# A hybrid token mixer on one core: weights kept split from the first block on, a second x tile, and zeroed tiles in the weight buffers

## The chip, the cores and the metric

One core of a Trainium2 chip runs the kernel. The metric is the device time of one execution in microseconds. The kernel before takes 2813.61 us in the median of three runs (2803.16 to 2818.05).

## The reference

One layer of a diffusion backbone, for 256 context tokens and 2048 latent tokens of width 1024, in float32. Each token is normalised and modulated by a condition, multiplied by w_in (1024 to 2560), and split into ten columns of 256 that feed four mixers; their outputs are multiplied by w_out, added to x with a gate, and an MLP of width 4096 with squared ReLU follows.

```python
def token_mixing(h, hg_s0, s5_s0_re, s5_s0_im, P, l):
    z = jnp.dot(h, P['w_in'][l])
    a_val, a_gate, g_u, g_v, h_q, h_i, h_g, h_ff, h_fb, s5_u = jnp.split(z, N_IN_BLOCKS, axis=-1)
    o_conv = conformer_conv(a_val, a_gate, ...)
    o_gm = chunk_gmlp(g_u, g_v, ...)
    o_hg, hg_end = hgrn_mixer(h_q, h_i, h_g, h_ff, h_fb, ...)
    o_s5, s5_re, s5_im = s5_mixer(s5_u, ...)
    mixed = jnp.concatenate([o_conv, o_gm, o_hg, o_s5], axis=-1)
    return jnp.dot(mixed, P['w_out'][l]), hg_end, s5_re, s5_im
...
    x = x + g1 * mix
    h = rms_norm(x, P['norm2_g'][l]) * (1.0 + sc2) + sh2
    x = x + g2 * jnp.dot(jnp.square(jax.nn.relu(jnp.dot(h, P['mlp_w1'][l]))), P['mlp_w2'][l])
```

The part that matters here is the hgrn mixer: a gated recurrence with a 64x64 state per head, run forward and backward. Its scores inside a chunk are q·k with a decay between the two positions.

## The kernel before

Tokens are cut into five blocks: block 0 holds the 256 context tokens, blocks 1 to 4 hold 512 latent tokens each. Activations lie with channels on the partitions. Every large product is made in split precision: a float32 operand is cut into a high part and a low rest, and three matmuls (hi·hi, hi·lo, lo·hi) add up; lines L192 to L194 (`gemm_cm`), L579 to L581 (`gemm_tm`) and L1114 to L1116.

A weight unit is 128 x 1024 numbers, 0.5 MB. It is loaded into a raw buffer (tile `wraw`, three buffers, L179), and split by ScalarE (L156, the high part) and GpSimd or VectorE (L160, L162, the rest) into a tile `whl` of 1 MB (four buffers). The first use writes the split tile to DRAM (`kept_unit`, L182); later uses read that (L176). w_p1t and w_p1c are the weights of the first pass, w_p2c and w_p2t those of the second.

The first pass takes the blocks in the order 1, 2, 3, 4, 0 (`P1_ORDER`). Block 1 has a function of its own (`first_block`, from L655), in which its products go along with the ada modulation, k slice by k slice: `load(k)` fetches a slice of the ada weights (tile `aw`, two buffers) and of the first weights, `ready(k)` computes the modulation of that slice (adaT, L657), modulates x and splits the weights. These eight splits take the first two units of w_p1c and all four of w_p1t; they are not kept. For each later block x is loaded, squared and its rms found (`pass1_x`, tile `x`; L240, L248, L252, L256, L289), `pass1_h` modulates and splits it, `pass1_t` makes four token-major tiles (v and the S5 input; tile `vt` has two buffers), and `pass1_g` makes three groups for each of two pairs of heads.

Each of the ten (block, pair) combinations has an hgrn chain, `hgrn_local`. It goes through seven levels in which the decays of neighbouring spans double their length: at each level ScalarE copies q into a zeroed tile (L794, L795), PE makes scores of q and kt (L762, 32 columns each), and VectorE and GpSimd multiply kt, q and the decays by neighbours (L804, L805, L806, L813). Levels 0 to 2 use three tiles `qz0` to `qz2` that all chains share and that are zeroed once (L1395); levels 3 to 6 use `qzr`, zeroed each time. Level 4 copies the scores of five levels by a mask (L820). A chain ends with transposes (L830), the product with v (L836) and the state contributions (L845). Chain i + 1 starts when chain i has done five steps, so two chains run interleaved. When all are done for a segment, `hgrn_states` runs the recurrence over chunks (L869, L872).

The second pass takes block 0 first and then 1 to 4; its first block loads w_p2c and w_p2t raw, splits them and keeps them: ten units. w_out and the MLP follow. A scheduler with a model of the engines turns the program into one fixed order per engine, before the kernel runs; the DMAs are all issued by SyncE (SP) in its own fixed order, and an SP row that waits for a semaphore holds up all rows behind it.

Of the kernel before, what the change touches and what calls it, by code (L numbers as in the profile page):

```python
# [10 lines left out]
F32 = mybir.dt.float32  # L11
F32R = mybir.dt.float32r
# [38 lines left out]
P1_ORDER = [1, 2, 3, 4, 0]  # L51
# [23 lines left out]
def trunk_kernel(ctx, tc, I, O):  # L75
# [31 lines left out]
    def f32(ap):  # L107
        return ap.bitcast(F32)
# [41 lines left out]
    def wtile():  # L150
        return wts.tile([128, 2, 1024], F32R, tag="whl", name=nm("whl"), bufs=4)
# [17 lines left out]

    kept = {}  # L170

    def kept_unit(name, i, pool_only=True, every=3, keep=True):

        t = wtile()
        if (name, i) in kept:
            SP.dma_start(f32(t), f32(kept[name, i]))  # L176
            return t[:, 0, :], t[:, 1, :]
        raw = wts.tile([128, 1024], F32, tag="wraw", name=nm("wraw"), bufs=3)
        SP.dma_start(raw, I[name][i])  # L179
        split_unit(raw, pool_only, every=every, t=t)  # L180
        kept[name, i] = dt_(f"{name}_hl{i}", [128, 2, 1024], F32R)
        SP.dma_start(f32(kept[name, i]), f32(t))  # L182
        return t[:, 0, :], t[:, 1, :]

    def gemm_cm(ps, n, unit, hs, ts=None):
# [18 lines left out]
    def dt_(name, shape, dt=F32):  # L204
        return dram.tile(shape, dt, tag=name, name=name)
# [363 lines left out]
        pass1_save(b, hs)  # L569
        return hs  # L570

    def pass1_x(b, xp):
        x8 = xblock(xp, b, w=512, halves=4)
        return x8, rms_rstd(xp, x8, BLOCKS[b][1], V)

    def gemm_tm(ps, w, xs, wh, wl, first, last):
# [83 lines left out]
    def first_block(b, adap, xp, hp, p1):  # L660


        t0, n, c = BLOCKS[b]
        m = n // CH
        w = 512 + 2 * 128

        def load(k):
            aw = adap.tile([128, 8, 256], F32, tag="aw", name=nm("aw"), bufs=2)
            SP.dma_start(aw, I["ada_w0"][k])
            raw = wts.tile([128, 1024], F32, tag="wraw", name=nm("wraw"), bufs=3)  # L670
            SP.dma_start(raw[:, 0:512], I["w_p1t"][k // 2][:, (k % 2) * 512:(k % 2) * 512 + 512])
            SP.dma_start(raw[:, 512:w].rearrange("p (u f) -> p u f", u=2),
                         I["w_p1c"][0:2, :, k * 128:(k + 1) * 128].rearrange("u p f -> p u f"))
            return aw, raw

        c32 = cond32(adap)
        x8 = xblock(xp, b, w=512, halves=4, engs=(V, G, V), pos=True)
        loads = [load(k) for k in range(4)]
        yield
        ps = pg()  # L680
        for k in range(0, 8, 2):
            sq = [xp.tile([128, 512], F32, tag=tag, name=nm("sq"), bufs=2) for tag in ("sq", "hm")]
            for i in range(2):
                A.activation(sq[i][:, :n], x8[:, k + i, :n], AF.Square)
            V.tensor_tensor(sq[0][:, :n], sq[0][:, :n], sq[1][:, :n], ALU.add)
            PE.matmul(ps[:, :n], ones, sq[0][:, :n], start=k == 0, stop=k == 6)
        rstd = rstd_of(ps, n, 1.0 / D_MODEL)
        yield
        pts, pcs = None, None
        hs, ws_ = [], []  # L690

        def ready(k):
            aw, raw = loads[k]
            ada_unit(pa(), (aw[:, 0:4], aw[:, 4:8]), c32, adap, slice(k, k + 9, 8))
            V.scalar_tensor_tensor(gs1[:, :, k], adaT[:, 8 + k, :], 1.0, n1g[:, k:k + 1].to_broadcast([128, 2]),
                                   ALU.add, ALU.mult)
            hs.append(modulate1(xp, hp, x8, n, rstd, gs1[:, c, :], adaT[:, 0:8, c], k))
            ws_.append(split_unit(raw, True, w))

        ready(0)  # L700
        for k in range(8):
            if k < 7:
                ready(k + 1)
            hi, lo = ws_[k]
            if k == 0:
                pts = [psums["w"].tile([128, 512], F32, tag="pw", name=nm("pw")) for _ in range(m - 1)] + [pg()]
                pcs = [pg(), pg()]
            for i in range(m):
                gemm_tm(pts[i], 512, [x[:, i * 128:(i + 1) * 128] for x in hs[k]], hi[:, 0:512], lo[:, 0:512],
                        k == 0, k == 7)  # L710
            for i in range(2):
                ws = slice(512 + 128 * i, 640 + 128 * i)
                PE.matmul(pcs[i][:, :n], hi[:, ws], hs[k][0][:, :n], start=k == 0, stop=False)
                PE.matmul(pcs[i][:, :n], hi[:, ws], hs[k][1][:, :n], start=False, stop=False)
                PE.matmul(pcs[i][:, :n], lo[:, ws], hs[k][0][:, :n], start=False, stop=k == 7)
            if k + 4 < 8:
                loads.append(load(k + 4))
        state0.append((b, pts, pcs, hs, p1))
# [599 lines left out]
    def pool(stack, name, bufs=1, side="left"):  # L1318
        return stack.enter_context(tc.tile_pool(name=name, bufs=bufs, side=side))
# [20 lines left out]
    with ExitStack() as e1:  # L1340
        p1a = pool(e1, "p1a")
        es = ExitStack()
        s5s = pool(es, "s5s")
        s5t = pool(es, "s5t")
        psum(es, t=1)
        with ExitStack() as ea:
            psum(ea, w=3)
            adap = pool(ea, "adap")
            hp = pool(e2, "hp", 8, side="right")
            ex = ExitStack()  # L1350
            xp = pool(ex, "xp", side="right")
            start = first_block(P1_ORDER[0], adap, xp, hp, p1a)
            step(start, 1)
            small = s5_small(s5s)
            more_consts()
            run(start)
            lower_bounds()
            first_out()
        hs, vt, gates = first
        with ExitStack() as e:  # L1360
            psum(e, u=3)
            s5_tables(s5t, scr, small)
        es.close()
        psum(e1, s=2)
        Sx = [spool.tile([128, 4, 4, 64], F32, tag="Sc", name="Sc"),
              spool.tile([128, 4, LAT // CH + 2, 64], F32, tag="Sl", name="Sl")]
        pre = pass1_x(P1_ORDER[1], xp)
        state = [hs, vt, pre]

        def prep(i):  # L1370

            b, pair = P1_ORDER[i // 2], i % 2
            if i == 0:
                g_ = gates
            else:
                if pair == 0:
                    state[1] = pass1_t(b, state[0], p1a)
                g_ = pass1_g(b, pair, state[0], p1a)
            vt = state[1]
            if pair == 1 and i // 2 + 1 < NB:  # L1380
                state[0] = pass1_h(P1_ORDER[i // 2 + 1], xp, hp, state[2])
                if i // 2 + 2 < NB:
                    state[2] = pass1_x(P1_ORDER[i // 2 + 2], xp)
                else:
                    ex.close()
            return g_ + (vt,)

        ready = [prep(0), prep(1)]
        p1 = pool(e1, "p1")
        masks_ = p1.tile([128, 5, 32], I32, tag="masks", name="masks")  # L1390
        for o_ in range(0, 128, 32):
            SP.dma_start(masks_[o_:o_ + 32], I["masks"][o_:o_ + 32, :, o_:o_ + 32])
        qz = [p1.tile([128, 1024], F32, tag=f"qz{lv}", name=f"qz{lv}") for lv in range(3)]
        for z in qz:
            G.memset(z, 0.0)  # L1395
        prev = None
        for i in range(2 * NB):
            cur = hgrn_local(P1_ORDER[i // 2], i % 2, *ready[i], p1, qz, Sx, masks_)
            for _ in range(5):
                step(cur)  # L1400
                if prev:
                    step(prev)
            prev = cur
            if i == 0:
                s5_kernels()
            if i + 2 < 2 * NB:
                ready.append(prep(i + 2))
        run(prev)
        hs = state[0]
        p2 = pool(e2, "p2", side="right")  # L1410
        gm = [const("gmg", [128, 256], I["gmlp_norm_g"], F32, p2, SP),
              const("gmw", [128, 4, 128], I["gmlp_ws"], F32, p2, SP),
              const("gmb", [128, 2, 128], I["gmlp_bs"], F32, p2, SP)]

        def all2():
            gates = []
            for b in P1_ORDER[-1:] + P1_ORDER[:-1]:
                for i, _ in enumerate(pass2(b, p2, hp, hs if b == P1_ORDER[-1] else None, Sx, gates, *gm)):
                    if i in DEFER and b != P1_ORDER[-1]:
                        hgrn_out(*gates.pop(0))  # L1420
                    yield
            for g_ in gates:
                hgrn_out(*g_)

        second = all2()
        step(second, 2)
# [88 lines left out]
    for b in range(1, NB):  # L1515
        x8, h2 = nxt
# [120 lines left out]
```

## Time and profile before

| | |
|---|---|
| median of three runs | 2813.61 us |
| the profiled execution: time, span | 2807.04 us, 2805.3 us |
| granted clock, mean | 0.968 |
| PE busy | 2628.2 us, 94% |
| VectorE (DVE) busy | 1818.5 us, 65% |
| ScalarE (ACT) busy | 1143.9 us, 41% |
| GpSimd (POOL) busy | 911.6 us, 32% |
| DMA | 467.35 MB, mean 167 GB/s |

The busy time of PE counts from the start of a matmul to its modelled end; matmuls overlap, so a sum over groups is more than the time they take. Shares of the whole span hide that the kernel has two halves: up to about 1050 us several engines and the DMA queues take turns in being the last, and after it PE hardly stops. To read a stage, cut it out with a window and see which engine is full there, and what the idle engine waits for.

### The profile page before, as it was taken

Reading aid. Unit: us, or ns where it says so; the run is one execution under the profiler, and the core shown is the slowest. Engines: PE = TensorE matmul, PEld = TensorE weight load, DVE = VectorE, ACT = ScalarE, POOL = GpSimd, SP = SyncE. Lnnn points to the kernel's source line nnn. Section 1 sums busy time; section 2 is a strip of 40 time slices with the busy share of each in tenths; the row PEclk is TensorE's granted clock in tenths of the full one; section 3 lists DMA queues with packets and bytes.
Section 4 is the critical chain, followed back from the end, with each engine's and each line's share of the span. In section 5 each row is a group of like instructions: output and inputs, shape, how many; then the busy total and the mean of one; then the engine's idle time right before and its main releaser. Section 6 shows DMA issues by size and latency. Waiting matters only on the chain.

```text
span 2805.3 us, 44442 instructions
## 1 busy us (share of the span) xinstructions
PE 2628.2 (94%) x17544; PEld 2185.3 (78%) x17544; DVE 1818.5 (65%) x2686; ACT 1143.9 (41%) x1830; POOL 911.6 (32%) x809
## 2 busy tenths in 40 slices
PE   6786989899999889999999999999999999999998
PEld 3665767777777679987788888788887888888888
DVE  9869677856698877569873485944575334643336
ACT  4645555532434545442432343233333223423323
POOL 4346234512534533342221342221432112421113
PEclk8898899899999989999999999999999999999999
DMA  7894556878986756542332343333343233233223
GB/s 265 286 302 155 203 194 198 293 256 307 318 283 228 230 201 202 161 144 83 113 112 92 130 148 113 99 105 115 107 161 100 96 98 128 98 122 100 95 97 128
DMA packets 186865, 467.35 MB, mean 167 GB/s; under 512 B 40864, under 2 KB 70688, under 8 KB 173600
## 3 DMA queue, kind: packets, MB, share of 16 engines
q1 hardware_dynamic: 184496, 463.32, 49.3%
q8 instruction: 139, 2.28, 0.3%
q10 hardware_dynamic: 2160, 1.18, 0.1%
q14 instruction: 70, 0.57, 0.1%
HBM read 383.23 MB, written 77.53 MB: 164 GB/s over the span
## 4 chain that ended last, share of the span: by engine, by line
PE 60%; DVE 11%; DMA 2%; ACT 1%; issue 1%; POOL 1%; SPq 0%; DVEq 0%; ACTq 0%; POOLq 0%
PE pg L193 19%; PE pg L194 19%; PE pg L192 19%; DVE x L1202 4%; DVE m L1013 1%; DVE whl L162 1%; DVE gg L1021 1%; DMA x<-in_xT_dram 0%; DVE sq L1030 0%; DMA x<-uD 0%; DVE lo L304 0%; DMA x<-mixD 0%; DVE pa L289 0%; DVE x L240 0%; DVE lo L1263 0%
## 5 line engine op out<-in xcount | busy, mean ns | idle before, releaser
L192 PE MATMUL pg<-hi,whl 128*128 128x512 f32 (+1 forms) x3488 | 1282.4, 370 | 18.3 <-DMA whl<-w_p1c_hl 5.5
L193 PE MATMUL pg<-lo,whl 128*128 128x512 f32 (+1 forms) x3488 | 1281.3, 368 | 5.1 <-DVE lo L1263 3.6
L194 PE MATMUL pg<-hi,whl 128*128 128x512 f32 (+1 forms) x3488 | 1278.9, 368 | 1.9 <-DVE whl L162 1.7
L160 POOL TENSOR_TENSOR whl<-wraw,whl 128x512 fp32r<-128x512 f32 (+1 forms) x296 | 428.4, 1468 | 1174.3 <-ACT whl L156 1126.4
L192 PEld LDWEIGHTS pg<-hi,whl 128*128 128x128 f32 x3488 | 662.8, 190 | 133.4 <-issue 7.5
L193 PEld LDWEIGHTS pg<-lo,whl 128*128 128x128 f32 x3488 | 662.8, 190 | 117.1 <-issue 8.2
L194 PEld LDWEIGHTS pg<-hi,whl 128*128 128x128 f32 x3488 | 662.3, 190 | 110.6 <-issue 4.6
L156 ACT ACTIVATE whl<-wraw 128x1024 fp32r<-128x1024 f32 (+1 forms) x396 | 415.5, 1051 | 577.6 <-PE pg L194 457.6
L162 DVE TENSOR_TENSOR whl<-wraw,whl 128x1024 fp32r<-128x1024 f32 x248 | 313.7, 1265 | 67.6 <-ACT whl L156 66.7
L1275 DVE SCALAR_TENSOR_TENSOR x<-pg,adaT,x 128x512 f32<-128x512 f32 (+1 forms) x168 | 111.8, 668 | 279.9 <-PE pg L194 279.4
L1260 DVE TENSOR_TENSOR t<-t 128x512 f32<-128x512 f32 (+1 forms) x160 | 113.5, 710 | 246.0 <-ACT t L1259 245.9
L1259 ACT ACTIVATE t<-pg 128x512 f32<-128x512 f32 (+1 forms) x160 | 88.3, 552 | 354.6 <-PE pg L194 354.5
L1202 DVE SCALAR_TENSOR_TENSOR x<-x,cvw 128x512 f32<-128x512 f32 (+1 forms) x300 | 218.8, 774 | 0.2
L1263 DVE TENSOR_TENSOR lo<-t,hi 128x512 fp32r<-128x512 f32 (+1 forms) x160 | 140.5, 879 | 35.6 <-ACT hi L1262 35.5
L804 POOL TENSOR_TENSOR kt<-kt,tnx 64x256 f32<-64x256 f32 (+1 forms) x120 | 94.8, 807 | 157.8 <-issue 116.3
L1262 ACT ACTIVATE hi<-t 128x512 fp32r<-128x512 f32 (+1 forms) x160 | 92.9, 581 | 88.3 <-DVE t L1260 88.3
L252 POOL TENSOR_TENSOR sq<-sq,sq 128x512 f32<-128x512 f32 (+1 forms) x56 | 87.2, 1558 | 122.8 <-ACT sq L248 122.8
L1243 DVE SCALAR_TENSOR_TENSOR x<-pg,adaT,x 128x512 f32<-128x512 f32 (+1 forms) x40 | 27.6, 691 | 105.8 <-PE pg L194 105.8
L804 DVE TENSOR_TENSOR kt<-kt,tnx 64x256 f32<-64x256 f32 (+1 forms) x120 | 59.3, 517 | 52.6 <-PE psc L762 51.8
L248 ACT ACTIVATE sq<-x 128x512 f32<-128x512 f32 (+1 forms) x120 | 65.8, 552 | 63.1 <-DVE sq L252 15.5
L303 ACT ACTIVATE hi<-hm,adaT 128x512 fp32r<-128x512 f32 (+1 forms) x72 | 49.6, 698 | 61.2 <-DVE hm L301 59.9
L304 DVE SCALAR_TENSOR_TENSOR lo<-hm,adaT,hi 128x512 fp32r<-128x512 f32 (+1 forms) x72 | 66.7, 942 | 6.1 <-ACT hi L303 5.2
(376 smaller groups left out, 2762.0 us busy)
## 6 DMA issues: line engine op xcount, KB each, us to landing
wraw<-in_mlp_w_dram SPq DMA_DIRECT2D x328, 512.0 KB, 3.5
whl<-w_p2c_hl SPq DMA_DIRECT2D x32, 1024.0 KB, 7.5
whl<-w_p1c_hl SPq DMA_DIRECT2D x22, 1024.0 KB, 8.5
wraw<-in_w_out_dram SPq DMA_DIRECT2D x40, 512.0 KB, 3.5
awt<-in_ada_w_dram SPq DMA_DIRECT2D x32, 512.0 KB, 6.1
whl<-w_p1t_hl SPq DMA_DIRECT2D x12, 1024.0 KB, 5.6
x<-in_xT_dram SPq DMA_DIRECT2D x16, 512.0 KB, 6.2
aw<-in_ada_w_dram SPq DMA_DIRECT2D x8, 1024.0 KB, 6.6
```

Source lines behind the costliest of these rows:

```text
L156: A.activation(hi[:, :w], raw[:, :w], AF.Copy)
L160: G.tensor_tensor(lo[:, h_], raw[:, h_], f32(hi[:, h_]), ALU.subtract)
L162: V.tensor_tensor(lo[:, :w], raw[:, :w], f32(hi[:, :w]), ALU.subtract)
L192: PE.matmul(ps[:, :n], wh, xh[:, ts], start=k == 0, stop=False)
L193: PE.matmul(ps[:, :n], wh, xl[:, ts], start=False, stop=False)
L194: PE.matmul(ps[:, :n], wl, xh[:, ts], start=False, stop=k == 7)
L804: eng.tensor_tensor(kv, kv, tb(lo_, hi_, 1 - half)[:, hs_, :], ALU.mult)
L1202: V.scalar_tensor_tensor(acc[i][:, :n], u2[:, i, k:k + n], cvw[:, i, k:k + 1], acc[i][:, :n], ALU.mult, ALU.add)
L1260: V.tensor_tensor(r, r, r, ALU.mult)
L1262: A.activation(hi, r, AF.Copy)
L1263: V.tensor_tensor(lo, r, f32(hi), ALU.subtract)
L1275: V.scalar_tensor_tensor(x8[:, o, ts], ps[:, :n], adaT[:, 40 + o, c:c + 1], x8[:, o, ts], ALU.mult, ALU.add)
```

## The change

Four things. (1) The eight splits of `first_block` are written to the kept tiles of w_p1t and w_p1c, in 24 pieces, so later blocks read these units. (2) `pass1_x` puts x8 alternately into a second pool `xq` and the old one. (3) The `pass1_t` of block 2 is called before the chains. (4) The three `qz` tiles are taken from the raw weight buffers (`wraw`, three buffers), and no longer from a pool of their own.

```diff
--- before.py
+++ after.py
@@ -169,6 +169,11 @@
 
     kept = {}
 
+    def kept_tile(name, i):
+        if (name, i) not in kept:
+            kept[name, i] = dt_(f"{name}_hl{i}", [128, 2, 1024], F32R)
+        return kept[name, i]
+
     def kept_unit(name, i, pool_only=True, every=3, keep=True):
 
         t = wtile()
@@ -178,8 +183,7 @@
         raw = wts.tile([128, 1024], F32, tag="wraw", name=nm("wraw"), bufs=3)
         SP.dma_start(raw, I[name][i])
         split_unit(raw, pool_only, every=every, t=t)
-        kept[name, i] = dt_(f"{name}_hl{i}", [128, 2, 1024], F32R)
-        SP.dma_start(f32(kept[name, i]), f32(t))
+        SP.dma_start(f32(kept_tile(name, i)), f32(t))
         return t[:, 0, :], t[:, 1, :]
 
     def gemm_cm(ps, n, unit, hs, ts=None):
@@ -569,8 +573,8 @@
         pass1_save(b, hs)
         return hs
 
-    def pass1_x(b, xp):
-        x8 = xblock(xp, b, w=512, halves=4)
+    def pass1_x(b, xp, xq):
+        x8 = xblock(xq, b, w=512, halves=4)
         return x8, rms_rstd(xp, x8, BLOCKS[b][1], V)
 
     def gemm_tm(ps, w, xs, wh, wl, first, last):
@@ -695,7 +699,12 @@
             V.scalar_tensor_tensor(gs1[:, :, k], adaT[:, 8 + k, :], 1.0, n1g[:, k:k + 1].to_broadcast([128, 2]),
                                    ALU.add, ALU.mult)
             hs.append(modulate1(xp, hp, x8, n, rstd, gs1[:, c, :], adaT[:, 0:8, c], k))
-            ws_.append(split_unit(raw, True, w))
+            t = wtile()
+            ws_.append(split_unit(raw, True, w, t=t))
+            SP.dma_start(f32(kept_tile("w_p1t", k // 2)[:, :, (k % 2) * 512:(k % 2) * 512 + 512]), f32(t[:, :, 0:512]))
+            for u in range(2):
+                SP.dma_start(f32(kept_tile("w_p1c", u)[:, :, k * 128:(k + 1) * 128]),
+                             f32(t[:, :, 512 + 128 * u:640 + 128 * u]))
 
         ready(0)
         for k in range(8):
@@ -1364,8 +1373,11 @@
         psum(e1, s=2)
         Sx = [spool.tile([128, 4, 4, 64], F32, tag="Sc", name="Sc"),
               spool.tile([128, 4, LAT // CH + 2, 64], F32, tag="Sl", name="Sl")]
-        pre = pass1_x(P1_ORDER[1], xp)
+
+        xqs = [pool(ex, "xq", side="right"), xp]
+        pre = pass1_x(P1_ORDER[1], xp, xqs[0])
         state = [hs, vt, pre]
+        early = []
 
         def prep(i):
 
@@ -1374,23 +1386,24 @@
                 g_ = gates
             else:
                 if pair == 0:
-                    state[1] = pass1_t(b, state[0], p1a)
+                    state[1] = early.pop() if early else pass1_t(b, state[0], p1a)
                 g_ = pass1_g(b, pair, state[0], p1a)
             vt = state[1]
             if pair == 1 and i // 2 + 1 < NB:
                 state[0] = pass1_h(P1_ORDER[i // 2 + 1], xp, hp, state[2])
                 if i // 2 + 2 < NB:
-                    state[2] = pass1_x(P1_ORDER[i // 2 + 2], xp)
+                    state[2] = pass1_x(P1_ORDER[i // 2 + 2], xp, xqs[(i // 2 + 1) % 2])
                 else:
                     ex.close()
             return g_ + (vt,)
 
         ready = [prep(0), prep(1)]
+        early.append(pass1_t(P1_ORDER[1], state[0], p1a))
         p1 = pool(e1, "p1")
         masks_ = p1.tile([128, 5, 32], I32, tag="masks", name="masks")
         for o_ in range(0, 128, 32):
             SP.dma_start(masks_[o_:o_ + 32], I["masks"][o_:o_ + 32, :, o_:o_ + 32])
-        qz = [p1.tile([128, 1024], F32, tag=f"qz{lv}", name=f"qz{lv}") for lv in range(3)]
+        qz = [wts.tile([128, 1024], F32, tag="wraw", name=f"qz{lv}", bufs=3) for lv in range(3)]
         for z in qz:
             G.memset(z, 0.0)
         prev = None
```

On SP the writes of (1) stand among the loads of the first block's raw slices and of aw: three for each of the eight units, which read that unit's split tile and wait for its split. Line numbers of the kernel after are 4 to 13 higher.

On PE at the end of block 3's third pass1_t tile, whose last products open each piece. Before:

```order
L581 MATMUL pg_3053<-whl_2992,hi_2542 128x512
L762 MATMUL psc_2613<-q_2604,kt_2603 32x32 x32
L762 MATMUL psc_2653<-qzr_2648,kt_2026 32x32 x32
L762 MATMUL psc_2701<-qz_1541,kt_2603 32x32 x32
L762 MATMUL psc_2747<-qzr_2742,kt_2026 32x32 x32
L762 MATMUL psc_2793<-qz_1542,kt_2603 32x32 x32
L762 MATMUL psc_2839<-qzr_2834,kt_2026 64x64 x16
L762 MATMUL psc_2867<-qz_1543,kt_2603 32x32 x26
L256 MATMUL pa_2598<-sq_2575,ones 128x512
L762 MATMUL psc_2867<-qz_1543,kt_2603 32x32 x6
L830 MATMUL psc_2909<-ident,kt_2026 128x128 x8
L836 MATMUL psc_2919<-at_2028,vt_837 64x128 x8
```

After (L771 is L762 before, L839 and L845 are L830 and L836):

```order
L585 MATMUL pg_3050<-whl_2989,hi_2539 128x512
L771 MATMUL psc_2698<-qz_1699,kt_2600 32x32 x32
L771 MATMUL psc_2744<-qzr_2739,kt_2023 32x32 x32
L771 MATMUL psc_2790<-qz_1700,kt_2600 32x32 x32
L260 MATMUL pa_3761<-sq_3738,ones 128x256
L771 MATMUL psc_2836<-qzr_2831,kt_2023 64x64 x16
L771 MATMUL psc_2864<-qz_1701,kt_2600 32x32 x32
L839 MATMUL psc_2906<-ident,kt_2023 128x128 x8
L845 MATMUL psc_2916<-at_2025,vt_867 64x128 x8
L771 MATMUL psc_2942<-qzr_2937,kt_2600 32x32 x29
L854 MATMUL psc_2916<-vt_867,kt_2023 128x64 x8
```

The chain stands two steps further on when the products end: the first scores (q, and the first qzr) now come ahead, and an rms sum of 256 columns stands where one of 512 stood. Up to the next product 270 scores follow one another before (208 in the rows shown, 62 behind them), and 198 after (173 and 25).

SP, the first load of a raw second-pass unit. Before, and with its waits:

```order
L563 DMA hD_101<-lo_1431 128x512 [waits DMAHW7_49,DVE_49]
L562 DMA hD_101<-hi_1436 128x512 [waits DMAHW0_49,Activation_49]
L563 DMA hD_101<-lo_1437 128x512 [waits DMAHW1_49,DVE_49]
L179 DMA wraw_6573<-in_w_p2c_dram 128x1024 [waits DMAHW2_49]
L562 DMA hD_101<-hi_1442 128x512 [waits DMAHW3_49,Activation_49]
```

After:

```order
L762 DMA q_6200<-qn_5834 64x256 [waits DMAHW0_49]
L762 DMA q_6200<-qn_5834 64x256 [waits DMAHW1_49]
L849 DMA oD_118<-at_5426 128x512 [waits DMAHW2_49,Activation_49]
L184 DMA wraw_6571<-in_w_p2c_dram 128x1024 [waits DMAHW3_49,PE_49,Activation_49]
L835 DMA qD_109<-q_5897 128x512 [waits DMAHW4_49,DVE_49]
L184 DMA wraw_6605<-in_w_p2c_dram 128x1024 [waits PE_49,Activation_49]
```

It moved from row 108 to row 309 and waits for PE and ACT, behind the last chains' stores.

PE, behind the last product of the first pass (pg_5867). After:

```order
L198 MATMUL pg_5867<-hi_4879,whl_5868 128x256
L771 MATMUL psc_5688<-qz_1701,kt_5424 32x32 x32
L839 MATMUL psc_5730<-ident,kt_4885 128x128 x8
L845 MATMUL psc_5740<-at_4887,vt_4157 64x128 x8
L771 MATMUL psc_5766<-qzr_5761,kt_5424 32x32 x32
L854 MATMUL psc_5740<-vt_4157,kt_4885 128x64 x8
L771 MATMUL psc_5906<-q_5897,kt_5896 32x32 x16
L771 MATMUL psc_5930<-qzr_5925,kt_5424 32x32 x32
```

The same place before, where products of the second pass (pg_6571) stand among the scores:

```order
L193 MATMUL pg_6571<-lo_4859,whl_6572 128x256
L194 MATMUL pg_6571<-hi_4858,whl_6572 128x256
L762 MATMUL psc_5690<-qz_1543,kt_5426 32x32 x32
L192 MATMUL pg_6571<-hi_4864,whl_6572 128x256
L193 MATMUL pg_6571<-lo_4865,whl_6572 128x256
L194 MATMUL pg_6571<-hi_4864,whl_6572 128x256
```

In the after order 312 scores and two chain ends follow one another, until the first second-pass product at row 1300.

## Rows read from the trace of the kernel before

**Rows 1.** Page: busy time, share of the span and instructions of each engine.
```profile
PE 2628.2 (94%) x17544; PEld 2185.3 (78%) x17544; DVE 1818.5 (65%) x2686; ACT 1143.9 (41%) x1830; POOL 911.6 (32%) x809
```

**Rows 2.** Windows, all engines; columns in the first line.
```profile
core 0: us, PE busy (x) PEld busy (x) DVE busy (x) ACT busy (x) POOL busy (x), PEclk, DMA share, GB/s
...
20.00:75.00 55.00, 40.36 (x238) 28.72 (x237) 53.39 (x201) 24.14 (x47) 26.11 (x22) 0.81 0.77 264
...
100.00:170.00 70.00, 55.62 (x242) 44.68 (x242) 46.64 (x60) 39.68 (x65) 30.99 (x25) 0.90 0.82 285
...
245.00:293.00 48.00, 25.14 (x679) 20.93 (x679) 43.44 (x72) 26.34 (x47) 28.99 (x32) 0.67 0.26 86
...
345.00:391.00 46.00, 38.25 (x753) 31.44 (x752) 44.30 (x85) 29.41 (x55) 22.42 (x28) 0.93 0.52 161
...
491.00:606.00 115.00, 95.17 (x1372) 82.63 (x1371) 88.95 (x223) 60.56 (x125) 51.79 (x82) 0.87 0.78 273
502.20:569.90 67.70, 52.26 (x942) 48.48 (x942) 59.57 (x148) 38.16 (x76) 34.09 (x55) 0.88 0.85 299
606.00:840.00 234.00, 222.44 (x1438) 179.07 (x1437) 173.76 (x285) 85.42 (x187) 82.72 (x92) 0.99 0.87 302
840.00:1050.00 210.00, 183.29 (x1270) 153.42 (x1270) 177.72 (x256) 104.45 (x207) 96.33 (x92) 0.91 0.65 218
1050.00:2805.00 1755.00, 1739.66 (x8354) 1461.52 (x8352) 991.08 (x1130) 622.40 (x843) 465.93 (x311) 1.00 0.36 118
```

**Rows 3.** Timeline of PE: start, duration, engine, line, names, [idle before <-releaser].
```profile
251.82 0.39 PE L581 MATMUL pg<-whl,hi 128*128 128x512 f32 x1
...
264.52 1.08 PE L762 MATMUL psc<-qz,kt 128*32 128x32 f32 x64 [10.67 <-ACT qz L795]
...
271.41 1.08 PE L762 MATMUL psc<-qz,kt 128*32 128x32 f32 x64 [4.95 <-ACT sq L248]
...
293.17 0.80 PE L579 MATMUL pg<-whl,hi 128*128 128x512 f32 x1
```

**Rows 4.** DVE groups, 253 to 287 us: busy us, mean ns, idle before.
```profile
L252 DVE TENSOR_TENSOR sq<-sq,sq 128x512 f32<-128x512 f32 x6 | 4.6, 764 | 0.0
L289 DVE RECIPROCAL rstd<-pa 128x512 f32<-128x512 f32 x1 | 3.3, 3342 | 0.0
```

**Rows 5.** Tile aw, 0 to 110 us: first and last start.
```profile
L647 PE MATMUL pa<-aw,c x128: 378/380/637, 17.0 to 83.3; 128*32 128x256 f32 x128
L669 SPq DMA_DIRECT2D aw<-in_ada_w_dram x8: 328/356/409, 5.6 to 67.1; - x8
```

**Rows 6.** DMA issues, 0 to 110 us: count, KB each, median us to landing.
```profile
aw<-in_ada_w_dram SPq DMA_DIRECT2D x8, 1024.0 KB, 6.6
...
wraw<-in_w_p1c_dram SPq DMA_DIRECT2D x8, 128.0 KB, 5.7
```

**Rows 7.** Tile qz, whole run: its memset; durations ns min/median/max, first and last start.
```profile
L1395 POOL MEMSET qz<- x3: 959/959/964, 159.5 to 161.3; 128x1024 f32 x3
```

**Rows 8.** DMA issues, 485 to 606 us, with the window's packets.
```profile
DMA packets 9428, 32.86 MB, mean 272 GB/s; under 512 B 1095, under 2 KB 2772, under 8 KB 7107
...
w_p2c_hl<-whl SPq DMA_DIRECT2D x8, 1024.0 KB, 4.9
```

**Rows 9.** DVE groups, 502.2 to 569.9 us.
```profile
L872 DVE SCALAR_TENSOR_TENSOR Sl<-Sl,tot 64x64 f32<-64x64 f32 x43 | 14.0, 363 | 0.6
...
L162 DVE TENSOR_TENSOR whl<-wraw,whl 128x1024 fp32r<-128x1024 f32 x3 | 3.7, 1226 | 0.1
L869 DVE SCALAR_TENSOR_TENSOR Sl<-Sl,tot 64x64 f32<-64x64 f32 x12 | 3.4, 304 | 2.5 <-ACT Sl L849 2.4
```

**Rows 10.** PE product groups, 502.2 to 569.9 us.
```profile
L192 PE MATMUL pg<-hi,whl 128*128 128x256 f32 (+1 forms) x61 | 19.1, 313 | 0.0
...
L1114 PE MATMUL pg<-whl,hi 128*128 128x256 f32 x16 | 5.2, 327 | 0.0
```


## The prediction

> **What bounds the kernel now.** I read the page first. TensorE (PE) is busy 2628.2 of 2805.3 us, 94% [rows 1]; the other 177 us are what there is to win. Then I cut the span into stages, to see where they lie. From 1050 us on PE is busy 1739.66 of 1755 us at full granted clock [rows 2]; nothing of the change touches that part, so only the first 1050 us can move. There PE's idle time is small in most stages and large in one: 245 to 293 us, where PE works 25.14 of 48 us, the clock falls to 0.67 and the DMA share to 0.26 [rows 2]. PE's timeline says what it is: after the product at 251.82 us only score matmuls (L762) of the hgrn chains, waiting for ACT and DVE steps, the longest 10.67 us, until the next product at 293.17, 41 us later [rows 3]. No product stands beside the chain there: the fourth tile of block 3's pass1_t cannot start before chain 1 has freed its v buffer. VectorE (DVE) is full in that hole (43.44 of 48 us), and in part with work that is not the chain's: block 4's squares, its reciprocal and x adds, the first two 4.6 + 3.3 = 7.9 us [rows 4]. The other stage to watch is 491 to 606 us, the end of the first pass: the last three chains run there with products of the second pass between them, PE 95.17 of 115 us, DMA share 0.78 [rows 2].
>
> **Part 1, the first weights kept split.** It adds 24 writes: 8 of 512 KB and 16 of 128 KB, 6.3 MB, as units 0 to 7 are split. It removes six raw loads of 0.5 MB and their splits, and six writes of 1 MB; it adds six reads of 1 MB. The splits that go lie on ACT and GpSimd (POOL) around 100 to 170 us, where neither is full (39.68 and 30.99 of 70 us) and PE idles 14.4 us [rows 2]: I take -1 us, bounds -6 and 0. The writes stand on SP's queue, each waiting for its split, and the later aw loads are queued behind them. The last aw load is issued at 67.1 us, PE's last matmul on it starts at 83.3 [rows 5], and a load lands in 6.6 us [rows 6], so about 9 us of delay are covered; if the last split (POOL, unit 7) ran later than that, each us would be PE's. Engine time: 20 to 75 us moves 264 GB/s at a share of 0.77, or 343 GB/s when busy; 6.3 MB take 18 us, and 55 x 0.23 = 12.7 us are free [rows 2]. The rest, 6 us, lies inside the 9. From above: a load of 128 KB takes 5.7 us to land beside 6.6 for 1024 KB [rows 6], so small pieces may cost twice their bytes: 8.4 MB, 24 us, 12 over, and of these at most about 10 reach PE. I take +2, bounds 0 and +10.
> The Trainium skill, DMA: Bandwidth & Descriptors, section Bandwidth, speaks against this part: transfers far under 1 MiB reach a fraction of the peak, a third at 64 KB against 78% at 1 MB. By an estimate from that table (128 KB at 43%, 512 KB at 68% of 436 GB/s) the writes take 25 us and not 18, 7 us more of the engines: by it the sum would be about 7 us higher, if nothing of it were covered, and rival D prices that case from rows. The landing times of [rows 6] lean the same way.
>
> **Part 2, a second x tile.** Block 3's and block 4's x, squares and rms run a block earlier (block 2's x lies where the ada weights lay and still waits for them). So the 7.9 us of block 4 leave the hole and block 0's half-width rms takes their place, about half. The waits of 10.67 and 4.95 us, the second behind ACT sq [rows 3], are what this work lengthens.
>
> **Part 3, block 2's first products ahead of the chains.** In the trace they ran there already; the position in program order changes little: 0.
>
> **Part 4, zeroed qz tiles in the raw buffers.** The memset ran at 159.5 us [rows 7], in a pool whose space came free only with the S5 tables' stores, and now need not wait for them; chain 0 can start some us earlier against the products. The order shows it: in the hole 198 scores are left bare in place of 270. With parts 2 and 4 together I price the hole by its waits: 10.67 and 4.95 us, 15.6, less what block 0's half rms still takes (about 4): -12, bounds 0 (the chain ends no earlier) and -20 (the 23 us of PE idle all but gone). 345 to 391 us has the same pattern with 7.8 us idle [rows 2]: -2, bounds -4 and 0.
> The price of part 4: qz holds all three raw buffers until the last chain has done its third level. Before, three raw loads of w_p2c stand long ahead on SP (rows 108, 159 and 160), and the split units flow out during chains 6 to 9: eight kept writes of w_p2c in 485 to 606 us, in 32.86 MB of all transfers [rows 8]. Now the first raw load is SP's row 309, and waits for PE and ACT; behind it stand q's store and reload, the other raw loads and the kept writes, all of block 0's second pass. On PE, 312 scores and two chain ends follow one another with no product between.
> How long is that bare stretch? Before, the same chain work is 502.2 to 569.9 us, 67.7 us, with DVE busy 59.57 [rows 2]. Of this L872 and L869 (states) take 17.4 and the splits L162 3.7 [rows 9]: 38.5 us are the floor, if the states' updates slip out of the way, and 59 the ceiling, if DVE is as full as before. The hole is the nearest row for a bare chain (DVE 91% busy, 43.44 of 48); the states of these chains stand inside the stretch, so I take the floor and L872's 14.0, 52 us. The chains come 67.7 - 52 = 15.7 us sooner, but the 182 + 48 products of that stretch (L192 to L194 and L1114 to L1116, one of each shown, [rows 10]) are still to do: a matmul of 512 columns costs 1739.66 / 8354 = 0.21 us at full clock [rows 2], 0.104 for 256 columns, 0.12 at 0.88, so 27 us. That is +11.
> Then block 0's second pass comes in one piece: ten units of 0.5 MB in and 1 MB out, 15.7 MB, at 299 / 0.85 = 352 GB/s [rows 2] 45 us, for 27 us of products: 18 us in which PE has only scores, and 491 to 606 us already holds 19.8 us of idle; I count +8. Against this, 606 to 1050 us has 11.6 + 26.7 = 38.3 us of PE idle [rows 2], where a PE that comes later can find its inputs ready sooner: -3. The end of the pass costs +16, bounds -5 (floor: 67.7 - 38.5 = 29 us sooner against 27, nothing for the DMA) and +32 (ceiling 59: +18, then +14).
>
> **The sum.** -1 + 2 - 12 - 2 + 16 = +3 us on the profiled 2807.04: 2810. That execution lies 6.6 us under the median of the three runs, 2813.61, so I put the forecast at 2817.
>
> **Rivals.**
> A, the forecast: gain at the front and loss at the pass's end nearly cancel, 2817, own range 2802 to 2831. Chance 0.44.
> B, faster: the bare stretch costs nothing. For it: DVE is the chain's bound in both places (59.57 of 67.7, 43.44 of 48), so chains without splits and products beside them run at DVE's floor, and the displaced products fill the 38 us of idle later. Against it: DMA is at 0.87 in 606 to 840 us, where they must go. Front -12 - 2 - 6, end -5, first block 0: -25, 2789. Chance 0.25.
> C, slower: the kept writes and the raw loads held back by qz. From the point where qz is free, the 15.7 MB and the reads of the next blocks meet a stage with only 0.13 x 234 = 30 us of free DMA time [rows 2]; when the transfers of 485 to 606 us (32.86 MB [rows 8], 0.78 x 121 = 94 us of the engines) shift by the 50 us of the bare stretch, PE waits for whl in 606 to 840 us. End +32, 240 products at the hole's clock of 0.67 in place of 0.88 [rows 2] (37 us and not 28) +10, front -12: +30, 2844. It decides as soon as the bare stretch is over 50 us with the DMA under 0.3 in it. Chance 0.23.
> D, the first block's writes: small packets fill the DMA engines and aw and raw come late: +10 there, and the hole stays as long as before, because the chain starts no sooner when the first block ends later. +10 - 2 + 8 = +16 (the end of the pass then gets half its price): 2830. Against it: 9 us of cover. It is also the case in which the change does not do at the front what it is described as doing. Chance 0.08.
>
> **Range and chances.** Under 0.5%, 14 us, a measurement of this kernel tells no change (three runs spread over 15 us). Range 2787 to 2846: B's and C's middles, with about 0.2 beyond. Faster by more: B and a little of A, 0.27; slower: C, D and a little of A, 0.32; no change, the rest of A, 0.41.
>
> **What would show it.** First block: aw loads landing ahead of use, and PE no later at block 2's first products than now. Hole: the stretch without products near 250 us is 27 to 32 us long in place of 41, with no wait of 10 us. End: a stretch of 45 to 59 us near 490 us with PE under half busy, granted clock low and DMA under 0.4; then block 0's products beside a DMA share over 0.85. B is right if PE's idle time in 491 to 1050 us is no more than the 58 us of now; C if it grows by 30 and whl or DMA is the releaser. I am wrong altogether if the stage after 1050 us is not the same length.

## The result, and the profile after

The changed kernel takes 2859.44 us (median of four runs, 2855.13 to 2859.82) against 2810.01 us before in the same comparison: a ratio of 1.0170, interval 1.0152 to 1.0187. It is slower by 49 us. The profiled execution has a span of 2853.3 us, 48 us longer, with a mean granted clock of 0.956 in place of 0.968.

The windows of the changed kernel, with the columns of [rows 2] (length, busy time of PE, weight loads, DVE, ACT, POOL, then clock, DMA share, GB/s):

```profile
20.00:75.00 55.00, 39.62 (x206) 27.96 (x204) 54.52 (x196) 22.61 (x44) 23.29 (x24) 0.81 1.00 338
...
245.00:293.00 48.00, 36.16 (x694) 29.76 (x692) 42.97 (x78) 28.19 (x52) 19.31 (x26) 0.82 0.46 153
...
491.00:548.00 57.00, 31.16 (x813) 27.21 (x813) 54.00 (x144) 33.55 (x71) 27.32 (x51) 0.59 0.15 48
502.50:547.90 45.40, 23.25 (x633) 20.18 (x633) 43.18 (x124) 24.60 (x53) 20.66 (x42) 0.56 0.16 54
548.00:606.00 58.00, 43.37 (x448) 39.08 (x448) 47.83 (x119) 26.08 (x54) 22.80 (x31) 0.88 0.96 339
606.00:640.00 34.00, 19.77 (x69) 12.98 (x69) 13.49 (x34) 2.42 (x4) 0.73 (x1) 0.74 1.05 389
606.00:840.00 234.00, 208.50 (x1283) 164.12 (x1287) 142.81 (x228) 69.19 (x153) 69.16 (x78) 0.94 0.83 291
840.00:1050.00 210.00, 191.91 (x1305) 157.28 (x1298) 160.08 (x238) 99.92 (x211) 87.03 (x88) 0.96 0.66 227
1050.00:2853.00 1803.00, 1777.27 (x8594) 1493.02 (x8592) 1022.13 (x1168) 642.24 (x872) 483.12 (x326) 0.99 0.37 122
```

PE does 17544 matmuls in both kernels. At 1050 us the changed one still has 8594 of them ahead, 240 more than before; at 0.21 us each, the mean of that stage in both kernels, these are some 50 us. Up to 491 us it has done 5101, and 5110 before. So the loss lies between the two. Three places have to be read.

First the front. In 20 to 75 us the DMA share is 1.00, where [rows 2] has 0.77, and the sum of squares of block 2 (PE's L260, L256 before) starts 14 us later. Its row in the timeline of PE after, and then before (start, duration, engine and line, names, count, idle before and releaser):

```profile
145.10 2.08 PE L260 MATMUL pa<-sq,ones 128*128 128x512 f32 x2 [0.45 <-DVE sq L256]
```

```profile
131.16 2.08 PE L256 MATMUL pa<-sq,ones 128*128 128x512 f32 x2 [2.48 <-DVE sq L252]
```

PE loses this time behind the stretch with the full DMA engines, in 66 to 110 us (window after, then before):

```profile
66.00:110.00 44.00, 27.50 (x146) 19.89 (x145) 31.27 (x73) 14.74 (x24) 11.89 (x10) 0.79 0.77 279
```

```profile
66.00:110.00 44.00, 38.35 (x218) 30.40 (x218) 40.93 (x90) 28.62 (x48) 17.70 (x12) 0.92 0.93 330
```

The DMA share is lower there than before, and PE's main wait (total, times, longest) is for the modulated x, not for a load:

```profile
PE pw L583 <- ACT hi L307: 11.0, 3, 5.9
```

Second the hole. PE's timeline after, from the last product to the next:

```profile
267.26 0.39 PE L585 MATMUL pg<-whl,hi 128*128 128x512 f32 x1
...
276.23 1.08 PE L771 MATMUL psc<-qz,kt 128*32 128x32 f32 x64 [6.73 <-DVE al L829]
...
284.73 1.94 PE L839 MATMUL psc<-ident,kt 128*128 128x128 f32 x8 [3.26 <-DVE kt L813]
...
294.29 0.80 PE L583 MATMUL pg<-whl,hi 128*128 128x512 f32 x1
```

It is 27 us long (267.3 to 294.3), where [rows 3] has 41, and the wait of 10.67 us in it is gone. But it ends at 294.3 us and not earlier than the 293.17 of [rows 3]: the 14 us won here are the 14 lost in the first block. Block 4's squares, which left it, stand now ahead of chain 0's first level (ScalarE makes them from 181.6 us on, and from 247.5 us on before); the waits of PE in 180 to 200 us (total, times, longest) show that:

```profile
PE psc L771 <- ACT qz L804: 8.7, 1, 8.7
```

From there the chains keep the old pace: the sixth ends at 475 us in both kernels, here with its last matmuls after, and then before. All of the 48 us come after it.

```profile
473.28 2.00 PE L854 MATMUL psc<-vt,kt 128*128 128x64 f32 x16
```

```profile
472.90 2.00 PE L845 MATMUL psc<-vt,kt 128*128 128x64 f32 x16
```

Third the end of the pass. PE has no product between these two:

```profile
500.01 0.41 PE L198 MATMUL pg<-hi,whl 128*128 128x256 f32 x1
...
547.86 0.58 PE L196 MATMUL pg<-hi,whl 128*128 128x256 f32 x1
```

That is the bare stretch, 47.5 us. In its last 45.4 us: PE 23.25 of 45.4 us, granted clock 0.56, DMA share 0.16, DVE 43.18 (the window of 502.5 us above). The first raw load of the second pass is issued in it, in SP's timeline behind the eighth chain's store:

```profile
531.10 0.33 SPq L849 DMA_DIRECT2D oD<-at  x1
540.48 0.34 SPq L184 DMA_DIRECT2D wraw<-in_w_p2c_dram  x1
```

Before, the first three were issued at these times:

```profile
146.89 0.64 SPq L179 DMA_DIRECT2D wraw<-in_w_p2c_dram  x1
...
185.51 1.28 SPq L179 DMA_DIRECT2D wraw<-in_w_p2c_dram  x2
```

Then everything comes at once. In 548 to 640 us the DMA moves this (packets of the window; then issues: count, KB each, median us to landing):

```profile
DMA packets 13913, 32.90 MB, mean 358 GB/s; under 512 B 2979, under 2 KB 7843, under 8 KB 11998
...
w_p2c_hl<-whl SPq DMA_DIRECT2D x8, 1024.0 KB, 7.0
...
w_p2t_hl<-whl SPq DMA_DIRECT2D x2, 1024.0 KB, 5.5
```

These are 32.90 MB in 92 us; [rows 8] has 32.86 MB in the 121 us of 485 to 606. The DMA share is 0.96 and 1.05 (packet times summed over 16 engines; here they overlap), and PE has no product from 595.8 us, when block 0's last one of this stage ends, to 618.4, when block 1's first begins. Its waits in 548 to 640 us:

```profile
PE pd L908 <- ACT uc L905: 11.6, 2, 10.9
PE pg L196 <- DMA hi<-hD: 9.8, 1, 9.8
```

uc waits for the S5 input of block 0 (tile zc), and hi<-hD is block 1's activations. SP issues them so, hi right behind the last kept write:

```profile
596.66 1.25 SPq L903 DMA_DIRECT2D zc<-s5uDc  x2
...
609.07 0.36 SPq L186 DMA_DIRECT2D w_p2c_hl<-whl  x1
609.53 0.38 SPq L1093 DMA_DIRECT2D hi<-hD  x1
```

Before, the first hi is issued at 556.1 us, long ahead, but zc only at 610.0, and PE waits 0.2 us for uc, because its order still has products ahead of it. So only hi is late against before. The same windows before, for comparison:

```profile
491.00:548.00 57.00, 45.12 (x760) 41.37 (x760) 52.79 (x105) 35.87 (x66) 37.57 (x47) 0.85 0.84 296
548.00:606.00 58.00, 50.05 (x614) 41.27 (x612) 36.16 (x119) 24.69 (x59) 14.22 (x35) 0.88 0.72 250
606.00:640.00 34.00, 33.76 (x223) 28.35 (x222) 20.52 (x49) 8.51 (x23) 1.60 (x5) 0.95 0.90 315
```

### The profile page after: what moved, and what is told of

The parts are those of the page before. It is cut to its first block, busy times and chain, and to the rows that moved or that the text cites. A ratio compares the mean times of both kernels' runs of the same rounds, so it can differ in the third digit from the quotient of the medians.

```text
span 2853.3 us, 44447 instructions
## 1 busy us (share of the span) xinstructions
PE 2646.8 (93%) x17544; PEld 2193.5 (77%) x17544; DVE 1804.8 (63%) x2686; ACT 1131.4 (40%) x1818; POOL 870.3 (31%) x797
## 4 chain that ended last, share of the span: by engine, by line
PE 56%; DVE 8%; DMA 2%; issue 1%; ACT 1%; POOL 0%; SPq 0%; DVEq 0%; ACTq 0%; POOLq 0%
PE pg L198 18%; PE pg L197 18%; PE pg L196 18%; DVE x L1211 2%; DVE whl L162 1%; DMA x<-uD 1%; DVE m L1022 1%; DVE lo L1272 0%; DMA t<-mixD 0%; DVE lo L308 0%; DVE gg L1030 0%; DVE x L244 0%; DVE t L1269 0%; DMA wraw<-in_mlp_w_dram 0%; PE pa L260 0%
## 5 line engine op out<-in xcount | busy, mean ns | idle before, releaser
L160 POOL TENSOR_TENSOR whl<-wraw,whl 128x512 fp32r<-128x512 f32 (+1 forms) x284 | 404.5, 1445 | 1194.4 <-ACT whl L156 1171.5
L156 ACT ACTIVATE whl<-wraw 128x1024 fp32r<-128x1024 f32 (+1 forms) x390 | 409.1, 1051 | 587.6 <-PE pg L198 455.7
L1272 DVE TENSOR_TENSOR lo<-t,hi 128x512 fp32r<-128x512 f32 (+1 forms) x160 | 140.3, 878 | 36.5 <-ACT hi L1271 36.4
L813 POOL TENSOR_TENSOR kt<-kt,tnx 64x256 f32<-64x256 f32 (+1 forms) x120 | 86.2, 737 | 144.1 <-issue 96.6
L256 POOL TENSOR_TENSOR sq<-sq,sq 128x512 f32<-128x512 f32 (+1 forms) x56 | 87.0, 1554 | 123.0 <-ACT sq L252 123.0
L1252 DVE SCALAR_TENSOR_TENSOR x<-pg,adaT,x 128x512 f32<-128x512 f32 (+1 forms) x40 | 27.7, 694 | 109.8 <-PE pg L198 109.7
L813 DVE TENSOR_TENSOR kt<-kt,tnx 64x256 f32<-64x256 f32 (+1 forms) x120 | 63.4, 557 | 36.4 <-PE psc L771 35.7
```

The source lines that it names most:

```text
L156: A.activation(hi[:, :w], raw[:, :w], AF.Copy)
L160: G.tensor_tensor(lo[:, h_], raw[:, h_], f32(hi[:, h_]), ALU.subtract)
L813: eng.tensor_tensor(kv, kv, tb(lo_, hi_, 1 - half)[:, hs_, :], ALU.mult)
L1272: V.tensor_tensor(lo, r, f32(hi), ALU.subtract)
```

## The experiments

Each ratio is to the kernel before, with its 95% interval. The theory in most of them: the three raw buffers that qz holds until the end of the pass cost most, and the transfers that pile up behind cost a good part of that. The scheduler makes a new order for each version, so rows move in other places too.

**The first weights kept, alone.** The kernel before, with the changed `first_block` writes and `kept_tile` and nothing else:

```diff
-            ws_.append(split_unit(raw, True, w))
+            t = wtile()
+            ws_.append(split_unit(raw, True, w, t=t))
+            SP.dma_start(f32(kept_tile("w_p1t", ...)...), f32(t[:, :, 0:512]))
...
```

> The kernel before with part 1 alone: first_block's eight splits are written to the kept tiles; one x tile, qz in its own pool, early call absent. The order at the end of the first pass is then that of before. Theory (the bare stretch of part 4 costs most, some 35 us, and the first block's writes about 14, of which the hole gives some back): 2815 to 2824 us, DMA share in 20 to 75 us near 1.00, the rms sum of block 2 near 145 us and not 131, and 491 to 606 us as in the kernel before. Rival (the first block's writes cause all 48 us): 2850 us or more.

Measured: 2816.74 us, 1.0016 (1.0000 to 1.0032). The time is inside the theory's range. The first block is delayed as in the changed kernel (block 2's sum of squares starts at 142.4 us), yet hardly 5 us are left at the end: the raw loads and splits of 100 to 170 us are gone, and the first chain ends only 4 us later than before (250.7 and 246.9 us). The end of the pass is that of before:

```profile
20.00:75.00 55.00, 40.01 (x214) 27.50 (x206) 54.01 (x199) 22.51 (x45) 22.84 (x22) 0.81 0.96 318
491.00:548.00 57.00, 45.28 (x831) 41.67 (x830) 52.88 (x99) 37.36 (x69) 38.79 (x46) 0.88 0.84 289
```

The rival falls: the writes do not make the 48 us.

**Without the second x tile.**

```diff
-        xqs = [pool(ex, "xq", side="right"), xp]
+        xqs = [xp, xp]
```

> The changed kernel without the second x tile: x8 always in the old pool. Theory: the bare stretch stays, and block 4's squares and reciprocal are back in the hole, 5 to 8 us: 2862 to 2868 us. Rival (the second x tile itself costs, by moving x loads into the busiest time of the DMA engines): 2840 to 2852 us.

Measured: 2852.29 us, 1.0153 (1.0129 to 1.0178). I had expected it to be slower than the changed kernel, and it is not; the time lies at the upper end of the rival's range. The interval overlaps the changed kernel's (1.0152 to 1.0187), so that the second tile costs something here is not shown either. It bears on the size of part 2, not on the loss.

**The first weights kept late.**

```diff
-            SP.dma_start(f32(kept_tile("w_p1t", ...)...), f32(t[:, :, 0:512]))
...
         early.append(pass1_t(P1_ORDER[1], state[0], p1a))
+        for i in range(2):
+            kept_unit("w_p1c", i)
```

> The changed kernel without the 24 writes in first_block: the four w_p1t units are loaded raw, split and written when block 2 needs them, and two units of w_p1c are loaded, split and written right behind, before the qz tiles take the raw buffers. qz in the raw buffers and the bare stretch stay. Theory: first block as before, rms sum of block 2 near 131 us, 8 to 14 us less than the changed kernel: 2845 to 2852 us. Rival (the first block's writes are the whole cause): 2810 to 2815 us.

Measured: 2857.49 us, 1.0172 (1.0147 to 1.0197). Both expectations missed: the first block is as before (block 2's sum of squares starts at 127 us), and nothing is won, because the six raw loads, splits and writes now stand ahead of the chains and the first chain ends at 259 us, 4 us later than in the changed kernel. Early or late, these writes cost about the same, and are not the cause.

**Two qz tiles in the raw buffers.**

```diff
-        qz = [wts.tile([128, 1024], F32, tag="wraw", ...) for lv in range(3)]
+        qz = [wts.tile([128, 1024], F32, tag="wraw", ...) for lv in range(2)]
```

> The changed kernel with two qz tiles in the raw buffers in place of three: level 2 uses a qzr tile that GpSimd zeroes each time, and one raw buffer is free for second-pass loads during the chains. In its order the 312 bare scores are gone, products of the second pass stand between them again. Theory (the held raw buffers cause the bare stretch, the transfers piling up behind it, and about 35 us): 2822 to 2834 us, DMA share in 500 to 548 us over 0.5 where the changed kernel has 0.15. Rival (chains are bound by VectorE there, the bare stretch costs nothing): 2854 to 2862 us.

Measured: 2828.62 us, 1.0075 (1.0051 to 1.0100): one free raw buffer gives back 31 us, in the middle of the theory's range. Windows, columns as above:

```profile
491.00:548.00 57.00, 40.07 (x832) 36.41 (x831) 53.95 (x123) 32.79 (x62) 34.44 (x54) 0.85 0.45 158
...
606.00:640.00 34.00, 27.31 (x161) 24.59 (x162) 24.46 (x57) 7.73 (x19) 1.64 (x2) 0.90 0.90 319
```

PE has 40 of 57 us in place of 31, and 27 of 34 in place of 20. The DMA share in 500 to 548 us is 0.47, a little under the 0.5 that I had set.

**No kept writes in the second pass.** Later blocks read kept tiles of the first pass.

```diff
-        SP.dma_start(f32(kept_tile(name, i)), f32(t))
+        if name.startswith("w_p1"):
+            SP.dma_start(f32(kept_tile(name, i)), f32(t))
...
```

> The changed kernel without the ten kept writes of the second pass (10 MB); the later blocks read kept tiles of the first pass in their place, so the output is not the reference's. qz stays in the raw buffers, the bare stretch stays. Theory 1 (the transfers that pile up behind the bare stretch, DMA share 0.96 to 1.05 in 548 to 640 us, cost about 25 of the 48 us): 2826 to 2838 us, PE busy over 28 of 34 us in 606 to 640. Theory 2 (the products that the bare stretch displaced are the whole price, because PE has no room to catch up): 2850 to 2860 us.

Measured: 2835.53 us, 1.0101 (1.0086 to 1.0116), 24 us less than the changed kernel. The bare stretch is unchanged and PE gains behind it:

```profile
491.00:548.00 57.00, 30.50 (x806) 26.55 (x804) 54.01 (x142) 33.80 (x70) 27.68 (x52) 0.60 0.13 44
548.00:606.00 58.00, 45.82 (x464) 42.41 (x464) 47.15 (x113) 27.77 (x56) 22.86 (x32) 0.82 0.71 230
606.00:640.00 34.00, 27.05 (x120) 22.07 (x121) 17.23 (x43) 2.46 (x4) 0.73 (x1) 0.71 0.90 324
```

In 606 to 640 us PE has 27.05 us, not over 28 as I wrote, and 19.77 in the changed kernel. The wait for block 1's activations (9.8 us) is gone. The wait for uc is not, so the writes are not its cause:

```profile
PE pd L912 <- ACT uc L909: 15.9, 3, 11.2
```

**The control**, the same omission in the kernel before:

> The kernel before without the ten kept writes of the second pass, later blocks reading first-pass kept tiles (output not the reference's): the control for the same omission in the changed kernel, which gave 23 us. Theory (there the writes hurt because they pile up behind the bare stretch; here they lie hidden beside chains): 2802 to 2810 us, within 8 us of before. Rival (the writes cost as much anywhere): 2784 to 2792 us.

Measured: 2812.34 us, 1.0007 (0.9994 to 1.0020), within the 8 us of before, though over the 2810 I gave. The 10 MB cost nothing there and 24 us here. It is the place of the writes, not the writes.

**No qz at all**, in the changed kernel, in that kernel without the first-block writes, and in the kernel before (all levels take the tile that is zeroed each time):

```diff
-        qz = [... for lv in range(3)]
+        qz = []
```

> The changed kernel with no qz tile at all: levels 0 to 2 take qzr tiles like the other levels, zeroed by GpSimd each time; the raw buffers are free all along, and the end of the pass is ordered with products among the chains as in the kernel before. Writes in first_block and the second x tile stay. Theory (held raw buffers are the price of the change): 2806 to 2820 us, 38 to 50 less than the changed kernel. Rival (the second x tile and the first writes cost 10 to 18 us on their own, seen in the kernel with two qz tiles as what is left): 2822 to 2832 us.

> As the kernel with no qz tile, and without the writes in first_block: the second x tile alone beside the early call. Theory: the hole near 250 us is shorter by the 8 us of block 4's squares and reciprocal, the first block is as before: 2798 to 2810 us. Rival (the second x tile gives nothing, as the pair with and without it beside the bare stretch says): 2810 to 2818 us.

> The kernel before with no qz tile, all levels zeroed by GpSimd each time (some 3 x 9 x 1.03 = 28 us more of GpSimd work in the chains), nothing else changed. It prices the zeroing alone: 2806 to 2816 us if GpSimd is off the chain's path, 2825 to 2835 if it is on it.

Measured: 2819.74 us, 1.0041 (1.0019 to 1.0063); 2812.88 us, 1.0015 (1.0005 to 1.0024); 2818.69 us, 1.0030 (1.0013 to 1.0048). With the raw buffers free the loss is gone but for 10 us, as the theory had it, at the upper end of its range; the kernel without first-block writes came out in its rival's range (2810 to 2818), so the second x tile wins little. Zeroing costs 0.3%, a little over the upper end I gave for it off the chain's path. The second x tile lowers that to 0.15%, and the first-block writes raise it to 0.41%; the intervals of neighbours overlap, so each of these steps of some 5 us is only likely.

**qz released after seven chains, and after eight.** qz stays where the change put it; only the last chains do without it.

```diff
-            cur = hgrn_local(..., p1, qz, Sx, masks_)
+            cur = hgrn_local(..., p1, qz if i < 7 else [], Sx, masks_)
```

> The changed kernel, qz still in the three raw buffers, but the last three chains (one of 512 tokens, two of 256) take qzr tiles at levels 0 to 2, so the raw buffers come free after the seventh chain's third level and not after the tenth's. Everything else as changed. Theory (it is when the raw buffers come free, not where qz lies): the bare stretch is gone, 2808 to 2818 us, 40 to 50 less than the changed kernel. Rival (without the three early raw loads the second pass still starts late and its transfers pile up): 2825 to 2840 us.

> As the kernel that releases qz after seven chains, but after eight (only block 0's two chains take qzr at levels 0 to 2). The raw buffers come free about one chain later, near 495 us. Theory: between the two, 2815 to 2830 us. If the price were a step (anything but the full hold costs nothing): 2808 to 2816 us.

Measured: after seven 2810.64 us, 0.9995 (0.9984 to 1.0006); after eight 2817.73 us, 1.0025 (1.0014 to 1.0036). Both are inside the ranges of their theories. This is the experiment that decides. All of the 49 us come back when the last three chains do without qz, and 42 of them when the last two do. With qz released after seven chains SP issues its first raw load at 454.8 us, not at 540.5 as in the changed kernel, and long after the 146.9 us of before:

```profile
454.83 0.53 SPq L184 DMA_DIRECT2D wraw<-in_w_p2c_dram  x1
```

```profile
491.00:548.00 57.00, 45.89 (x799) 42.30 (x799) 52.70 (x101) 35.44 (x66) 45.10 (x58) 0.91 0.82 285
...
606.00:640.00 34.00, 33.31 (x197) 27.63 (x196) 22.41 (x57) 7.23 (x18) 1.14 (x4) 0.90 0.96 339
```

These windows read like those of before. So three raw loads long ahead are worth nothing that these runs can tell; what counts is that raw buffers are free while the last three chains run. One chain more costs 7 us, three more (the changed kernel) 49.

**The late writes, released after six.**

> The changed kernel with the first weights written late (as in the experiment that moved the writes behind block 2's products) and the last four chains on qzr at levels 0 to 2. What is left of the change is the second x tile and qz in raw buffers for six chains. If the second x tile gives 6 us, as the pair of kernels without qz says, and the first-block writes cost 6: 2802 to 2812 us. If the late writes cost as much as the early ones, as beside the bare stretch: 2808 to 2818 us.

Measured: 2817.42 us, 1.0030 (1.0013 to 1.0046): the second of the two cases, at its upper end. No version here is faster than the kernel before; the one released after seven chains is level with it.

## Why the prediction was wrong

The forecast was 2817 us, within 0.5% of before; measured were 2859.44. The step that failed is the price of the end of the pass in part 4: +16 us, bounds -5 and +32. Measured it is all of the 48, since the sixth chain still ends at the same time in both kernels. In the sum's own terms: the displaced products stood there at 27 us, the sooner chains at -15.7, the transfers at +8 and the catching up at -3. By these pieces:

- The bare stretch was there, from 500 us on, 47.5 us long, between the floor of 38.5 and the 52 that I took, with DVE full. The eighth chain ends at 535 us and not at 555: the chains did come some 20 us sooner, and B's first half (the chains are bound by DVE) was right.
- The DMA term was mis-sized: +8, worked out as engine time of ten units against idle that was there already. Taking 10 MB of writes out gives 24 us, and none before. What I left out is what stands behind these transfers in SP's one queue: PE's wait of 9.78 us is for block 1's activations, and it goes with the writes. The longer one, 10.86 us for block 0's S5 input, stays without them: PE's order has no product left to do ahead of it. Where the rest of the 24 us lies is not shown.
- The term of -3 cannot be read from 606 to 1050 us as one: PE's idle time there is 43.6 us after and 38.3 before, but 14.2 of the 43.6 lie in 606 to 640 us, in the heap, and 0.2 before. From 640 us on it is 29.4 against 38.0, though the same window holds different work in the two kernels. That PE catches up a little later is thus not refuted.
- The displaced products run behind the bare stretch, up to 606 us at a clock of 0.88, the one that I had taken; that their 27 us were too few is not shown. With the 24 us of the writes they make 51, so that nothing of the credit of 15.7 us for the sooner chains is seen in the time: where the chains were over, PE waited. That is a sum and not an experiment; no run here parts products, clock and order.
- The low clock of the bare stretch (0.56) is a quarter at most. From 491 us to the end PE's idle time grows from 73.4 to 109.8 us, 36.4, and its busy time, in which a slower clock shows, from 2240.6 to 2252.2, 11.6.

The front was right in the hole and wrong in the first block. The hole shrank from 41 to 27 us, as forecast (27 to 32). The first block lost 14 us where I took +2, bounds 0 and +10. The loads landed later, aw in 8.1 us and not 6.6, but the cover of 9 us was there: the last aw load is issued at 71.6 us and has landed by 81, and PE comes to it at 101.3. PE waits there for the modulation on DVE and ScalarE, and DVE once 8.2 us for PE. It comes with the writes, since with the first weights kept late the block is as before; whether through the order that the scheduler then makes or through the transfers is open.

```profile
aw<-in_ada_w_dram SPq DMA_DIRECT2D x6, 1024.0 KB, 8.1
w_p1t_hl<-whl SPq DMA_DIRECT2D x8, 512.0 KB, 6.8
w_p1c_hl<-whl SPq DMA_DIRECT2D x16, 128.0 KB, 6.7
```

The hole and the first block cancel in the chains' times, so that the front's gain was near nothing and not 13.

Of the rule on small transfers (the Trainium skill, DMA: Bandwidth & Descriptors, section Bandwidth) the trace bears out little. From [rows 2] to the window after, 20 to 75 us takes 0.23 x 55 = 12.7 us more of the engines for 74 GB/s x 55 us = 4.1 MB more, 322 GB/s beside the 343 of before, where by the rule's estimate of 25 us for the 6.3 MB it would be 252 GB/s. The landing times, 6.7 us for 128 KB and 6.8 for 512 KB, hardly depend on the size, so they do not price it.

Rival C came nearest: raw loads held back and transfers in one heap. It had the end at +32 and +10, 42 in all, and the front at -12; with the front at nothing it would have said 2856. That this is so near is in part luck: its +10 was for slower products, and it had PE waiting for whl, where PE waits 1.8 us for whl and 9.8 for hi. Its sign was a bare stretch over 50 us with the DMA under 0.3; measured are 47.5 us and 0.16. Its chance was 0.23, too low: I had the order in front of me, and weighed it against a gain at the front that rested on the first block's cover. Rival B is out: PE's idle time in 491 to 1050 us is 84 us, not 58. Of D the number for the first block came true (+14 for +10), its reason did not: PE waits for no late aw. The hole did not stay as long as before, but it ends no sooner, as D had it.

## What to carry to other kernels

Before a tile is moved into another pool's buffers, ask until when it is held, and what that pool feeds next: here the same move costs 49 us or nothing, by whether the last three of ten users hold on to it. When transfers are pushed back, price not only their own engine time but every load that stands behind them in the same queue, and the stage that first reads it. Ask also whether the engine that waits would have had other work: here the same load costs 0.2 us before and 10.9 after, because the products were gone. A gain and a loss in front of a chain whose pace is fixed elsewhere meet at that chain: compare its step times in both traces before adding them up.

## What the runs showed of the hardware

The ten kept writes of the second pass, 10 MB, cost 24 us when they come in one heap with other transfers and nothing when they are spread beside compute (1.0007, 0.9994 to 1.0020). The DMA engines went up to 389 GB/s in 606 to 640 us of the changed kernel, against 315 in the same stretch before; the share shown was then 1.05.
